# Three of nine dense column blocks in split fp32r parts, and every gathered dot beside the dense products: an expert mixer on one core

## The chip, the cores and the metric

The kernel runs on 1 core of one Trainium2 chip. Engines: PE (TensorE, matrix products), PEld (its weight loads), DVE (VectorE), ACT (ScalarE), POOL (GpSimd, which here issues the gathers by index), SP (SyncE, which issues the plain loads and stores). The metric is the device time of one execution in microseconds (us), as the median of several runs; lower is better. A time on the trace counts from the span's start.

## The reference, cut to what matters

One decoder layer for 256 prompt tokens and 32 sample tokens: an RWKV-7 and a sparse-attention token mixer, a norm, then a product-key expert mixer (PEER) and a last norm. The change lies in the PEER part of the prompt tokens, and in the last norm of the sample tokens:

```python
def peer_ffn(x, wq, subkeys, u_tab, v_tab):
    q = (xt @ wq).reshape(n, P_HEADS, 2, P_DKEY // 2)
    s = jnp.einsum('nhcd,hckd->nhck', q, subkeys)
    hv, hix = lax.top_k(s, P_TOPK)
    ...
    expert = jnp.take_along_axis(cand_e, tpos, axis=-1)
    gate = jax.nn.softmax(tv, axis=-1)
    h = jax.nn.gelu(jnp.einsum('cd,chkd->chk', xb, u_tab[eb]), approximate=False)
    return jnp.einsum('chk,chkd->cd', gb * h, v_tab[eb])
```

Each token chooses 8 x 16 = 128 of 16384 experts. For each it needs the dot product of its 2048 features with the expert's row of `peer_u`, a GELU, a gate, and then the sum of the experts' rows of `peer_v`, weighted by these.

## The kernel before, in words

All in one program: projections, RWKV chunks and attention first, then the queries and the choice of the experts, and from 1187.9 us (the first dense product) the three stages that matter here.

**Dense products beside dots.** The 2048 columns of `peer_u` are split. The last 9 blocks of 128 (`NDB = 9`) are taken densely: `dense(i1)` loads the rows of 128 experts, transposed, into a tile `ur` of 9 blocks (ring of `NUR = 5`), makes nine f32 products against the token features `Xfd` (128 x 256 each) into one PSUM bank `ph`, and ScalarE copies the result into a large table `AW`, which so holds, for each prompt token, the partial dot with every expert. There are 128 such steps. The first 7 blocks (`UG` = 896 columns) are taken by gather: `fetch` has POOL gather, for one slot of each of 128 tokens, the chosen expert's 896 columns into a tile of the ring `rows` (`NRW = 5`), and `dot` has VectorE multiply it with the tokens' features `X1a` and add up. There are 2 x 128 = 256 such dots, in two halves of 128 tokens. The loop asks for 1 or 2 dots per step (7 of 8 steps ask for 2), and what is left over after 128 steps is put into the first `NDL = 12` steps of the next stage. A gather waits until the dot five before it has released its tile.

**Spread sums.** 68 steps, pipelined over 64 groups of four tokens: `pick` builds one-hot rows (`oo`) on VectorE and transposes them on TensorE, `picked` multiplies `AW` with them to read out the chosen experts' partial dots, `product_of` reduces these on VectorE, `gated` applies gate and GELU, `scaled` scales the one-hots, `put` writes the weights back into `AW`. `table(t)` makes, for one half of the tokens, the transposed tables of indices, gates and gathered dots (`TB`) that `pick` needs. Beside it the sample tokens' experts are gathered whole (`smp_fetch`) and added up on TensorE (`smp_add`, weights `ws`), 32 times; after the loop their last norm follows, and 16 small stores.

**V products.** 128 blocks of 128 rows of `peer_v`: 1408 columns densely in split fp32r products, the other 640 by gather and VectorE.

The order on each engine is set by the framework's scheduler from a simulated time line, where nothing else fixes it. `keep_in_program_order` (`pin`) puts an instruction behind the one written just before it on its engine, and `issue_after` behind a given one. Each engine then works strictly in its order. Pools are stacks: `dp` (the dense tiles) and `kc` lie where `x4p` (the spread sums' tiles, `ws` and `oo` among them) comes later, and `up` (with `rows`, `x1a`) where the V products' tiles come; a tile in reused memory waits for the old one's last reader.

A split product writes each f32 operand as a rounded fp32r part plus its rest, and adds three of the four products of parts; the projections, the output projection and the V products do this already (lines 417 to 424, 1655 to 1661, 2059 to 2067).

Of the kernel before, what the change touches and what calls it, by code (L numbers as in the profile page):

```python
# [10 lines left out]
F32 = mybir.dt.float32  # L11
F32R = mybir.dt.float32r
I32 = mybir.dt.int32
U32 = mybir.dt.uint32
AF = mybir.ActivationFunctionType
OP = mybir.AluOpType
AX = mybir.AxisListType
PSUM = bass.MemoryType.PSUM
P = 128
# [3 lines left out]
NPR = 256  # L23
NEG = -1e30
ALPHA = 2.0 ** 0.25
# [23 lines left out]
NP1 = 8  # L49
NDW = 1  # L50
ND = 1
NDN = 7
NDL = 12
NUR = 5
NRW = 5
NDB = 9
UG = 128 * (16 - NDB)
WF = 3
PRO = 400
# [91 lines left out]
def hybrid_decode_step(ctx: ExitStack, tc: tile.TileContext, a, outs, dbg=None):  # L151
    nc = tc.nc
    ve, sc, pe, gp, sy = nc.vector, nc.scalar, nc.tensor, nc.gpsimd, nc.sync
# [35 lines left out]
    def bank(tag="pb"):  # L189
        places = [(pool, nm, n) for _, div in psum for t_, pool, nm, n in div for _ in range(n) if t_ == tag]  # L190
        turn[tag] = k = (turn.get(tag, -1) + 1) % len(places)
        pool, nm, n = places[k]
        return pool.tile([P, 512], F32, name=tag, tag=nm, bufs=n)
# [1248 lines left out]
    def norm_quarters(pool, x_, g_, b_, tag):  # L1442

        st, mv, rr, sq_ = pool([P, 6], "sst"), pool([P, 2], "smv"), pool([P, 1], "srr"), pool([P, 1], "ssq")
        ve.bn_stats(out=st, in_=x_)
        ve.bn_aggr(out=mv, in_=st)
        ve.tensor_tensor(sq_, mv[:, 0:1], mv[:, 0:1], OP.mult)
        ve.tensor_tensor(mv[:, 1:2], mv[:, 1:2], sq_, OP.add)
        pb = bank(tag)
        pe.matmul(pb[:, :2], C0("avg4"), mv, start=True, stop=True)  # L1450
        ve.tensor_copy(mv, pb[:, :2])
        ve.tensor_tensor(sq_, mv[:, 0:1], mv[:, 0:1], OP.mult)
        ve.tensor_tensor(mv[:, 1:2], mv[:, 1:2], sq_, OP.subtract)
        norm_row(pool, mv, rr)
        sc.activation(x_, x_, AF.Identity, bias=mv[:, 0:1], scale=rr)
        ve.tensor_tensor(x_, x_, g_, OP.mult)
        ve.tensor_tensor(x_, x_, b_, OP.add)
# [313 lines left out]
    TB = up([P, 4, NPR], "TB")  # L1771
    dp, kc, kq = (Pool(nm, "left") for nm in ("dp", "kc", "kq"))
    dp([P, NDB, P], "ur", bufs=NUR)
    Xfd = dp([P, NDB, NPR], "Xfd")
    SKT = kq([P, 16, P], "SKT")
    QP = kq([P, 16, NPR], "QP")

# [11 lines left out]
    def dot(n=1, upto=2 * P, keep=False, ahead=NRW):  # L1789

        for i in range(got[1], min(got[1] + n, upto)):
            t, s_ = dots[i]
            fetch(min(i + ahead, upto))
            r_, h_ = rows_.pop(i), HD[t][:, s_:s_ + 1]
            i_ = ve.scalar_tensor_tensor(r_, r_, 1.0, X1a[t], op0=OP.mult, op1=OP.mult, accum_out=h_)  # L1795
            if keep:
                tc.keep_in_program_order(i_)
            got[1] = i + 1

    def table(t):  # L1800

        pb = bank("pb")
        for q, (op_, v_) in enumerate(((OP.logical_shift_right, 7), (OP.bitwise_and, 127))):
            ii = up([P, P], "ii", I32)
            iff = ii.bitcast(F32)
            ve.tensor_scalar(ii, GI[t], v_, None, op0=op_)
            ve.tensor_copy(iff, ii)
            pe.transpose(pb[:, 128 * q:128 * q + 128], iff, ident)
        pe.transpose(pb[:, 256:384], GE[t], ident)
        pe.transpose(pb[:, 384:], HD[t], ident)  # L1810
        sc.copy(TB[:, :, P * t:P * t + P], pb.rearrange("p (a b) -> p a b", a=4))
# [36 lines left out]
        sample_formed()  # L1848
    sq_.close()
    kw_.close()  # L1850
    for q in range(0, NDB, 3):
        sc.copy(Xfd[:, q:q + 3, :], XT[:, 16 - NDB + q:19 - NDB + q, :])
    xq.close()
    kq.close()
    M_("peer")
# [6 lines left out]
    def dense(i1):  # L1862

        w = dp([P, NDB, P], "ur", bufs=NUR)
        sy.dma_start(w.rearrange("p k e -> p (k e)"), a["peer_u_t"][P * i1:P * i1 + P, :])
        ph = bank("ph")
        for e in range(NDB):
            mm = pe.matmul(ph[:, :NPR], w[:, e, :], Xfd[:, e, :], start=(e == 0), stop=(e == NDB - 1))  # L1868
        return mm, sc.copy(AW[:, i1 // 64, :, i1 % 64], ph[:, :NPR])  # L1869

    tabled = []
    for i1 in range(P):
        mm, end = dense(i1)
        n_ = ND + (i1 * NDN % 8 < NDN)
        dot(min(max(P - got[1], 0) or n_, n_))
        if got[1] >= P + 8 and not tabled:
            with tc.issue_after(mm.ins), tc.issue_after(end.ins):
                table(0)
            tabled.append(0)
    kc.close()  # L1880
    dp.close()
    if not tabled:
        dot(P - got[1])
        table(0)
    x4p, vr = Pool("x4", "left"), Pool("vr", "right")
    ig, vh2 = [GI[2], IG], vtab.rearrange("n (q c) -> (n q) c", q=2)
    banks(pt=2, px=2, pa=2, pb=1, fs=1)
# [60 lines left out]

    x4p([P, 4, P], "oT", bufs=2)
    ws = x4p([P, 32, 32], "ws")  # L1950
    ve.tensor_tensor(ws, C0("sum4")[:, None, :32].to_broadcast([P, 32, 32]), GE[2][:, :, None].to_broadcast([P, 32, 32]), OP.mult)
    fs, sr = bank("fs"), {}

    def smp_fetch(j):
# [5 lines left out]
    def smp_add(j):  # L1960
        for c in range(4):
            pin(pe.matmul(fs[32 * c:32 * c + 32, :], ws[:, j, :], sr[j, c // 2][:, 512 * (c % 2):512 * (c % 2) + 512],  # L1962
                          start=(j == 0), stop=(j == 31)))

    raw = {}

    def rows_load(k):

        raw[k] = (vp if k % 3 else vr)([P, FD], "v_", bufs=2 if k % 3 else 1)
        return sy.dma_start(raw[k], vtab[P * k:P * k + P, :FD])  # L1970

    left = 2 * P - got[1]
    for s_ in range(68):
        if s_ == 30:
            table(1)
        oT = pick(s_) if s_ < 64 else None
        if 3 <= s_ < 66 and s_ % 2:
            gated(s_ // 2 - 1)
        if s_ >= 4:
            put(s_ - 4)  # L1980
        if 0 <= s_ - 3 < 64:
            scaled(s_ - 3)
        if oT is not None:
            picked(s_, oT)
        if 0 <= s_ - 1 < 64:
            product_of(s_ - 1)
        if s_ < NDL:
            dot(-(-left * (s_ + 1) // NDL) + 2 * P - left - got[1], keep=True)
        for j in range(32):
            if s_ == NDL + j * (62 - NDL) // 32:  # L1990
                smp_fetch(j)
        for j in range(32):
            if s_ == NDL + 2 + j * (62 - NDL) // 32:
                smp_add(j)
        if s_ == 46:
            bs_, gs_, x_ = (xa_[:, 512 * n:512 * n + 512] for n in range(3))
            for q in range(4):
                r_, c_ = slice(32 * q, 32 * q + 32), slice(512 * q, 512 * q + 512)
                sy.dma_start(x_[r_, :], X1D[NPR:NT, c_])
                for t_, nm in ((gs_, "ln2_g"), (bs_, "ln2_b")):  # L2000
                    sy.dma_start(t_[r_, :], bass.AP(tensor=a[nm].tensor, offset=a[nm].offset + 512 * q, ap=[[0, 32], [1, 512]]))
        if s_ == 50:
            rows_load(0)
    pb = bank("pb")
    for t in range(2):
        pe.transpose(pb[:, 128 * t:128 * t + 128], TB[:, 2, P * t:P * t + P], ident)
        sc.copy(GE[t], pb[:, 128 * t:128 * t + 128])

    ve.scalar_tensor_tensor(x_, x_, ALPHA, fs, op0=OP.mult, op1=OP.add)
    norm_quarters(x4p, x_, gs_, bs_, "pb")  # L2010
    for q in range(4):
        for i in range(4):
            sy.dma_start(outs[1][:, i, 512 * q:512 * q + 512], x_[32 * q + 8 * i:32 * q + 8 * i + 8, :])
    x4p.close()
    up.close()
    banks(pj=2, pb=6)
# [136 lines left out]
```

## Time and profile before

| | |
|---|---|
| time, median of 3 runs | 2479.08 us (2474.55 to 2487.72) |
| the profiled execution | 2475.65 us |
| its span, mean granted TensorE clock | 2473.9 us, 0.95 |
| PE / PEld busy | 2255.7 us (91%) / 1886.1 us (76%) |
| DVE / ACT / POOL busy | 1745.4 us (71%) / 820.4 us (33%) / 1336.1 us (54%) |
| HBM read over the span | 665.69 MB |

How to read the lines: a group has line, engine, operation, tiles written <- tiles read, shape, and the count; then busy time in us, mean ns of one, and the engine's idle time before them, with what ended it. f32 matmuls show twice their number, since one is carried out in two passes. A window row has its bounds and length in us, each engine's busy time with its count of instructions, the granted clock (1.00 is full), the mean busy share of the 16 DMA engines, and GB/s; where windows of one line are asked for, only the engines that it runs on appear. A wait names the engine and tile that waited, and whom it waited for, with the total in us, the times, and the longest. A row of the timeline has start and duration in us.

### The profile page before, as it was taken

Reading aid. Unit: us, or ns where it says so; the run is one execution under the profiler, and the core shown is the slowest. Engines: PE = TensorE matmul, PEld = TensorE weight load, DVE = VectorE, ACT = ScalarE, POOL = GpSimd, SP = SyncE. Lnnn points to the kernel's source line nnn. Section 1 sums busy time; section 2 is a strip of 40 time slices with the busy share of each in tenths; the row PEclk is TensorE's granted clock in tenths of the full one; section 3 lists DMA queues with packets and bytes.
Section 4 is the critical chain, followed back from the end, with each engine's and each line's share of the span. In section 5 each row is a group of like instructions: output and inputs, shape, how many; then the busy total and the mean of one; then the engine's idle time right before and its main releaser. Section 6 shows DMA issues by size and latency. Waiting matters only on the chain.

```text
span 2473.9 us, 42694 instructions
## 1 busy us (share of the span) xinstructions
PE 2255.7 (91%) x15628; PEld 1886.1 (76%) x15628; DVE 1745.4 (71%) x3985; ACT 820.4 (33%) x1591; POOL 1336.1 (54%) x1419
## 2 busy tenths in 40 slices
PE   7979999997988997789999999995899799999996
PEld 7867898885645665578888888884777688888885
DVE  5789766555563446889856545556877799998888
ACT  3433222223341433220111111111777444443443
POOL 5678423233345005578666644655444588886672
PEclk9999999998896996899999999997999899999998
DMA  7777986449478984798699989995666699999994
GB/s 218 229 236 225 284 216 177 119 143 278 171 243 252 316 302 146 288 321 267 213 400 404 398 329 401 383 393 169 181 209 197 242 369 363 363 362 362 345 358 187
DMA packets 327602, 684.09 MB, mean 277 GB/s; under 512 B 82270, under 2 KB 200992, under 8 KB 326464
## 3 DMA queue, kind: packets, MB, share of 16 engines
q1 hardware_dynamic: 246176, 342.58, 41.7%
q0 software_dynamic: 81216, 338.78, 38.2%
q8 instruction: 123, 2.02, 0.3%
q14 instruction: 87, 0.71, 0.1%
HBM read 665.69 MB, written 23.88 MB: 279 GB/s over the span
## 4 chain that ended last, share of the span: by engine, by line
PE 46%; issue 14%; DVE 13%; POOL 11%; DMA 8%; ACT 2%; SPq 1%; POOLq 0%; DVEq 0%; ACTq 0%
PE pb L2067 19%; POOL rows L455 8%; PE pj L424 6%; PE pa L1661 3%; PE px L1910 2%; PE p L1081 2%; DVE sr L1557 2%; PE pa L1943 2%; DMA big<-in_state_rwkv 1%; PE ss L1498 1%; DMA co<-in_cache_cmp_kv,gidx 1%; PE pt L1902 1%; PE fs L1962 1%; DMA rows<-in_peer_u_g,gi 1%; DVE CA L478 1%
## 5 line engine op out<-in xcount | busy, mean ns | idle before, releaser
L1868 PE MATMUL ph<-Xfd,ur 128*128 128x256 f32 x2304 | 497.8, 379 | 0.0
L1868 PEld LDWEIGHTS ph<-Xfd,ur 128*128 128x128 f32 x2304 | 437.4, 190 | 59.5
L455 POOL DMA_INDIRECT rq<-in_peer_v_g,gi x256 | 378.5, 1479 | 142.0 <-DVE fP L2040 86.7
L455 POOL DMA_INDIRECT rows<-in_peer_u_g,gi x256 | 292.5, 1143 | 229.8 <-DVE rows L1795 199.5
L1795 DVE SCALAR_TENSOR_TENSOR rows<-rows,x1a 128x896 f32<-128x896 f32 x256 | 280.2, 1098 | 178.4 <-DMA rows<-in_peer_u_g,gi 178.0
L424 PE MATMUL pj<-XH,wl 128*128 128x288 f32 (+1 forms) x752 | 231.7, 308 | 14.9 <-DVE wl L419 8.5
L424 PE MATMUL pj<-XH,wh 128*128 128x288 f32 (+1 forms) x752 | 229.5, 305 | 15.2 <-DVE ss L754 6.9
L2040 DVE SCALAR_TENSOR_TENSOR fP<-rq,ge,fP 128x640 f32<-128x640 f32 x254 | 223.7, 881 | 5.7 <-DMA rq<-in_peer_v_g,gi 3.3
L424 PE MATMUL pj<-XL,wh 128*128 128x288 f32 (+1 forms) x752 | 225.9, 301 | 0.0
L2067 PE MATMUL pb<-vl,ah 128*128 128x512 f32 (+1 forms) x768 | 207.6, 378 | 1.3 <-DVE vl L2060 0.5
L1869 ACT COPY AW<-ph 128x256 f32<-128x256 f32 x128 | 77.2, 610 | 396.6 <-PE ph L1868 391.5
L2067 PE MATMUL pb<-vh,ah 128*128 128x512 f32 (+1 forms) x768 | 188.0, 380 | 22.1 <-ACT vh L2059 22.1
L2067 PE MATMUL pb<-vh,al 128*128 128x512 f32 (+1 forms) x768 | 205.8, 376 | 0.0
L417 ACT CAST wh<-wraw 128x512 fp32r<-128x512 f32 (+1 forms) x188 | 114.8, 616 | 228.9 <-PE pj L424 175.6
L2067 PEld LDWEIGHTS pb<-vh,ah 128*128 128x128 f32 x768 | 145.5, 196 | 44.9 <-ACT vh L2059 25.7
L478 DVE SCALAR_TENSOR_TENSOR CA<-co,wbc,CA 128x256 f32<-128x256 f32 x248 | 133.4, 575 | 48.7 <-DMA co<-in_cache_cmp_kv,gidx 48.7
L424 PEld LDWEIGHTS pj<-XH,wl 128*128 128x128 f32 (+1 forms) x752 | 143.8, 191 | 26.8 <-DVE wl L419 12.5
L2067 PEld LDWEIGHTS pb<-vl,ah 128*128 128x128 f32 x768 | 144.9, 195 | 24.2 <-DVE vl L2060 5.1
L424 PEld LDWEIGHTS pj<-XH,wh 128*128 128x128 f32 (+1 forms) x752 | 144.1, 192 | 21.4 <-DVE ss L754 7.3
L2067 PEld LDWEIGHTS pb<-vh,al 128*128 128x128 f32 x768 | 145.3, 195 | 19.4
L424 PEld LDWEIGHTS pj<-XL,wh 128*128 128x128 f32 (+1 forms) x752 | 144.2, 192 | 1.5 <-issue 1.2
L419 DVE TENSOR_TENSOR wl<-wraw,wh 128x512 fp32r<-128x512 f32 (+1 forms) x141 | 101.8, 731 | 44.4 <-ACT wh L417 43.8
(844 smaller groups left out, 4339.2 us busy)
## 6 DMA issues: line engine op xcount, KB each, us to landing
ur<-in_peer_u_t SPq DMA_DIRECT2D x128, 576.0 KB
wraw<-in_w_in SPq DMA_DIRECT2D x152, 256.0 KB
cw<-in_w_out SPq DMA_DIRECT2D x32, 512.0 KB
wraw<-in_w_out SPq DMA_DIRECT2D x32, 512.0 KB
wraw<-in_peer_wq SPq DMA_DIRECT2D x32, 512.0 KB
cw<-in_peer_wq SPq DMA_DIRECT2D x32, 512.0 KB
wraw<-in_w_in SPq DMA_DIRECT2D x64, 128.0 KB
co<-in_state_win_kv SPq DMA_DIRECT2D x16, 512.0 KB
```

Source lines behind the costliest of these rows:

```text
L417: sc.copy(wh[:, :, :n], w[:, :, :n])
L419: i_ = en.tensor_tensor(wl[:, :, :n], w[:, :, :n], wh[:, :, :n].bitcast(F32), OP.subtract)
L424: last[2] = pe.matmul(pb[:n, :nt], wi[:, k, :n], xi[(o + k) // 8][:, (o + k) % 8, :nt], start=(o + k == 0 and wi is wh and xi is xh), stop ...
L455: gp.indirect_dma_start(out=dst, out_offset=None, in_=rows_, in_offset=bass.IndirectOffsetOnAxis(ap=ix, axis=0))
L478: ve.scalar_tensor_tensor(d_, x_, w_, d_, op0=OP.mult, op1=OP.add)
L1081: pe.matmul(pb[hs[c], 64 * m:64 * m + 64], lhs(hs[c], m), rhs(hs[c], m), start=True, stop=True)
L1661: pe.matmul(acc[t], xi[:, e, P * t:P * t + P], wi[:, e, :], start=(k == e == n_ == 0), stop=(k == 6 and e == 1 and n_ == 2))
L1795: i_ = ve.scalar_tensor_tensor(r_, r_, 1.0, X1a[t], op0=OP.mult, op1=OP.mult, accum_out=h_)
L1868: mm = pe.matmul(ph[:, :NPR], w[:, e, :], Xfd[:, e, :], start=(e == 0), stop=(e == NDB - 1))
L1869: return mm, sc.copy(AW[:, i1 // 64, :, i1 % 64], ph[:, :NPR])
L2040: ve.scalar_tensor_tensor(fP[t], r_, w_, fP[t], op0=OP.mult, op1=OP.add)
L2067: pe.matmul(acc[3 * t + q][:, :n_], wi[:, P * t:P * t + P], xi[:, 512 * q:512 * q + n_], start=(k == 0 and wi is ah and xi is vh), stop=(k ...
```

## The change

Four things are altered together.

1. From step `NFB = 16` on, the first `NSP = 3` of the nine blocks of a dense step are computed as split products: ScalarE rounds the three weight blocks to fp32r, VectorE subtracts to get the rest (pinned), and nine fp32r matmuls follow the six f32 ones in the same bank. The token features get parts `XHd` and `XLd`. The ring `ur` shrinks from 5 to 3, and a ring `uhl` of 3 holds the parts.
2. The dots: 1 or 2 in turn for the first 16 steps, then 2 per step and pinned; the six left over come right behind the loop. None remain in the spread sums. `table(0)` is made once 152 dots are asked for, with four `ii` tiles in place of one; `table(1)` in step 20 in place of 30.
3. `ws` is made in step 1 of the spread sums, pinned, and the 32 additions of the sample lie in steps 3 to 58 in place of 14 to 62.
4. The sample's last norm and stores are issued in step 60 in place of after the loop.

```diff
-NDN = 7
-NDL = 12
-NUR = 5
+NDN = 8
+NUR = 3
+NSP = 3
+NFB = 16
...
-    Xfd = dp([P, NDB, NPR], "Xfd")
+    Xfd = dp([P, NDB - NSP, NPR], "Xfd")
+    XHd, XLd = dp([P, NSP, NPR], "XHd", F32R), dp([P, NSP, NPR], "XLd", F32R)
+    Xed = dp([P, NSP, NPR], "uhl", bufs=3)
...
-            ii = up([P, P], "ii", I32)
+            ii = up([P, P], "ii", I32, bufs=4)
...
-    for q in range(0, NDB, 3):
-        sc.copy(Xfd[:, q:q + 3, :], XT[:, 16 - NDB + q:19 - NDB + q, :])
+    for q, t_ in enumerate((Xed, Xfd[:, :3], Xfd[:, 3:])):
+        sc.copy(t_, XT[:, 16 - NDB + 3 * q:19 - NDB + 3 * q, :])
+    sc.copy(XHd, Xed)
...
-        for e in range(NDB):
-            mm = pe.matmul(ph[:, :NPR], w[:, e, :], Xfd[:, e, :], start=(e == 0), stop=(e == NDB - 1))
+        for e in range(NSP, NDB):
+            pe.matmul(ph[:, :NPR], w[:, e, :], Xfd[:, e - NSP, :], start=(e == NSP), stop=False)
+        if i1 < NFB:
+            for e in range(NSP):
+                mm = pe.matmul(ph[:, :NPR], w[:, e, :], Xed[:, e, :], start=False, stop=(e == NSP - 1))
+        else:
+            hl = dp([P, 2, NSP, P], "uhl", F32R, bufs=3)
+            sc.copy(hl[:, 0], w[:, :NSP, :])
+            tc.keep_in_program_order(ve.tensor_tensor(hl[:, 1], w[:, :NSP, :], hl[:, 0].bitcast(F32), OP.subtract))
+            for e in range(NSP):
+                for wi, xi in ((0, XHd), (0, XLd), (1, XHd)):
+                    mm = pe.matmul(ph[:, :NPR], hl[:, wi, e, :], xi[:, e, :],
+                                   start=False, stop=(e == NSP - 1 and wi == 1))
...
-    tabled = []
     for i1 in range(P):
+        if i1 == NFB:
+            ve.tensor_tensor(XLd, Xed, XHd.bitcast(F32), OP.subtract)
         mm, end = dense(i1)
-        n_ = ND + (i1 * NDN % 8 < NDN)
-        dot(min(max(P - got[1], 0) or n_, n_))
-        if got[1] >= P + 8 and not tabled:
+        n_ = ND + (i1 % 2 if i1 < NFB else 1)
+        dot(min(max(P - got[1], 0) or n_, n_), keep=i1 >= NFB)
+        if got[1] == P + 24:
             with tc.issue_after(mm.ins), tc.issue_after(end.ins):
                 table(0)
-            tabled.append(0)
...
+    def sample_out():
+
+        ve.scalar_tensor_tensor(x_, x_, ALPHA, fs, op0=OP.mult, op1=OP.add)
+        norm_quarters(x4p, x_, gs_, bs_, "pb")
+        for q in range(4):
+            for i in range(4):
+                sy.dma_start(outs[1][:, i, 512 * q:512 * q + 512], x_[32 * q + 8 * i:32 * q + 8 * i + 8, :])
+
...
-    left = 2 * P - got[1]
+    dot(2 * P - got[1])
+    at = lambda j: 2 + 55 * j // 31
+    bs_, gs_, x_ = (xa_[:, 512 * n:512 * n + 512] for n in range(3))
     for s_ in range(68):
-        if s_ == 30:
+        if s_ == 20:
             table(1)
...
-        if s_ < NDL:
-            dot(-(-left * (s_ + 1) // NDL) + 2 * P - left - got[1], keep=True)
+        if s_ == 1:
+            pin(ve.tensor_tensor(ws, C0("sum4")[:, None, :32].to_broadcast([P, 32, 32]),
+                                 GE[2][:, :, None].to_broadcast([P, 32, 32]), OP.mult))
         for j in range(32):
-            if s_ == NDL + j * (62 - NDL) // 32:
+            if s_ == at(j) - 1:
                 smp_fetch(j)
         for j in range(32):
-            if s_ == NDL + 2 + j * (62 - NDL) // 32:
+            if s_ == at(j) + 1:
                 smp_add(j)
-        if s_ == 46:
-            bs_, gs_, x_ = (xa_[:, 512 * n:512 * n + 512] for n in range(3))
+        if s_ == 24:
...
+        if s_ == 60:
+            sample_out()
...
-    ve.scalar_tensor_tensor(x_, x_, ALPHA, fs, op0=OP.mult, op1=OP.add)
-    norm_quarters(x4p, x_, gs_, bs_, "pb")
-    for q in range(4):
-        for i in range(4):
-            sy.dma_start(outs[1][:, i, 512 * q:512 * q + 512], x_[32 * q + 8 * i:32 * q + 8 * i + 8, :])
```

More of the change, by code (lines that the diff above doesn't have):

```diff
@@ L1866, in dense @@
         ph = bank("ph")
-        for e in range(NDB):
-            mm = pe.matmul(ph[:, :NPR], w[:, e, :], Xfd[:, e, :], start=(e == 0), stop=(e == NDB - 1))
+        for e in range(NSP, NDB):
[11 more added lines that the diff above has]
+                                   start=False, stop=(e == NSP - 1 and wi == 1))
         return mm, sc.copy(AW[:, i1 // 64, :, i1 % 64], ph[:, :NPR])
-    tabled = []
     for i1 in range(P):
+        if i1 == NFB:
+            ve.tensor_tensor(XLd, Xed, XHd.bitcast(F32), OP.subtract)
         mm, end = dense(i1)
-        n_ = ND + (i1 * NDN % 8 < NDN)
-        dot(min(max(P - got[1], 0) or n_, n_))
-        if got[1] >= P + 8 and not tabled:
+        n_ = ND + (i1 % 2 if i1 < NFB else 1)
+        dot(min(max(P - got[1], 0) or n_, n_), keep=i1 >= NFB)
+        if got[1] == P + 24:
             with tc.issue_after(mm.ins), tc.issue_after(end.ins):
                 table(0)
-            tabled.append(0)
     kc.close()
     dp.close()
-    if not tabled:
-        dot(P - got[1])
-        table(0)
     x4p, vr = Pool("x4", "left"), Pool("vr", "right")
@@ L1950, in hybrid_decode_step @@
     ws = x4p([P, 32, 32], "ws")
-    ve.tensor_tensor(ws, C0("sum4")[:, None, :32].to_broadcast([P, 32, 32]), GE[2][:, :, None].to_broadcast([P, 32, 32]), OP.mult)
     fs, sr = bank("fs"), {}
```

## The prediction

> **What bounds the kernel now.** All durations are from one profiled execution, 2475.65 us with a span of 2473.9 us. I read the page first, then the stretch of the dense products.
>
> ```profile
> L1868 PE MATMUL ph<-Xfd,ur 128*128 128x256 f32 x2304 | 497.8, 379 | 0.0
> L1868 PE MATMUL ph<-Xfd,ur x2304: 379/379/382, 1187.9 to 1685.4; 128*128 128x256 f32 x192
> L1795 DVE SCALAR_TENSOR_TENSOR rows<-rows,x1a 128x896 f32<-128x896 f32 x256 | 280.2, 1098 | 178.4 <-DMA rows<-in_peer_u_g,gi 178.0
> L1795 DVE DVE_READ_ACCUMULATOR rows<-rows,x1a 128x1 f32 x256 | 21.1, 83 | 0.0
> ur<-in_peer_u_t SPq DMA_DIRECT2D x128, 576.0 KB
> ```
>
> TensorE never stands here: 2304 matmuls in 497.8 us, 216 ns each, two per f32 block of 256 columns, so 18 x 216 = 3.89 us per step. A dot takes VectorE 1.098 + 0.083 = 1.18 us, but it waits for gathered rows. The windows of the dots' line give, for each stretch, its length, VectorE's busy time in dots, their instructions (two per dot), granted clock, DMA share and GB/s:
>
> ```profile
> 1187.00:1220.00 33.00, 3.12 (x3) 1.00 0.55 177
> 1220.00:1250.00 30.00, 13.82 (x26) 1.00 0.97 363
> 1250.00:1300.00 50.00, 29.71 (x54) 1.00 1.01 400
> 1300.00:1450.00 150.00, 88.97 (x162) 1.00 1.01 399
> 1450.00:1500.00 50.00, 18.25 (x35) 1.00 0.86 311
> 1650.00:1686.00 36.00, 6.59 (x12) 1.00 0.56 216
> 1686.00:1712.30 26.30, 19.29 (x35) 0.63 0.75 248
> 1712.30:1755.00 42.70, 14.32 (x28) 0.83 0.57 171
> ```
>
> The DMA engines are full (share 1.01, 399 to 400 GB/s) and give a dot every 50 / 27 = 1.85 us. So two things are tight together: TensorE, and transfers. By 1686 some 225 of 256 dots are done; (35 + 28) / 2 = 31 are left, and they hold the spread sums until 1755. Two of the holes in the transfers have names in the waits and the timeline of VectorE:
>
> ```profile
> DVE ii L1806 <- PE pb L1808: 23.4, 3, 16.5
> 1678.06 1.23 DVE L1951 TENSOR_TENSOR ws<-CT,ge 128x1024 f32<-128x1024 f32 x1 [18.17 <-PE ph L1868]
> 1680.21 1.22 DVE L1898 TENSOR_TENSOR oo<-CT,TB 128x1024 f32<-128x1024 f32 x1
> 1712.44 1.22 DVE L1898 TENSOR_TENSOR oo<-CT,TB 128x1024 f32<-128x1024 f32 x1
> 1915.65 1.22 DVE L1898 TENSOR_TENSOR oo<-CT,TB 128x1024 f32<-128x1024 f32 x1
> ```
>
> The single `ii` buffer holds VectorE 16.5 us (the 0.86 window), and `ws`, in memory of the dense tiles, 18.2 us (the 0.56 window); dots queue behind both. Step 2 of the spread sums picks only at 1712.44, 27 us after the dense end; the last of 64 picks is at 1915.65.
>
> **The change part by part.** *The split.* From step 16 on, 6 blocks stay f32, 12 x 216 = 2.59 us, and three become nine fp32r matmuls of 256 columns. The nearest rows are the projection's fp32r matmuls of 288 columns, TensorE's timeline at full clock:
>
> ```profile
> 40.03 0.30 PE L424 MATMUL pj<-XH,wh 128*128 128x288 f32 x1
> 40.16 0.29 PE L424 MATMUL pj<-XL,wh 128*128 128x288 f32 x1
> ...
> 41.09 0.29 PE L424 MATMUL pj<-XH,wl 128*128 128x288 f32 x1
> ```
>
> Eight starts in 1.06 us, 133 ns. By columns 256 take 118; 133 is the upper end, and I take 120: 9 x 120 = 1.08 us in place of 6 x 216 = 1.30. A step falls to 3.67 us (3.65 to 3.79).
>
> *What it adds to ScalarE and VectorE.* A cast and a subtraction of 128x384 per step. Rows of the same two operations:
>
> ```profile
> L417 ACT CAST wh<-wraw 128x512 fp32r<-128x512 f32 x184 | 112.8, 618 | 228.2 <-PE pj L424 175.6 <-DMA wraw<-in_w_in 38.9 <-issue 5.0
> L419 DVE TENSOR_TENSOR wl<-wraw,wh 128x512 fp32r<-128x512 f32 x138 | 100.2, 735 | 44.4 <-ACT wh L417 43.8
> L1656 DVE TENSOR_TENSOR wl<-wraw,wh 128x1024 fp32r<-128x1024 f32 x24 | 30.8, 1284 | 21.5 <-ACT wh L1655 21.4
> L1869 ACT COPY AW<-ph 128x256 f32<-128x256 f32 x128 | 77.2, 610 | 396.6 <-PE ph L1868 391.5 <-DVE HV L1364 5.1
> ```
>
> The line through 735 and 1284 ns gives 0.60 us for 384 elements. VectorE then has 2 x 1.18 + 0.60 = 2.96 us a step, ScalarE at most 0.61 + 0.62: both fit under 3.67, at no cost while they are not held by a wait.
>
> *Transfers per step.* 576 KiB of columns (590 kB) and now two gathers of 128 x 896 x 4 bytes (917 kB): 1507 kB, at 399 GB/s 3.78 us. This is above 3.67, so transfers set the pace, and a faster TensorE alone brings nothing.
>
> *The new order.* From step 16 each subtraction is pinned behind the dots of the step before, on VectorE, and TensorE's split matmuls wait for it. Step 17's stands behind 28 dots (2 ahead of the loop, 24 of the first 16 steps, 2 of step 16). TensorE ends step 15 at 1187.9 + 16 x 3.89 = 1250.1, when (3 + 26) / 2 = 14 dots are done. Fourteen more at 1.85 us, or at 26.3 / 17.5 = 1.50 us as in 1686 to 1712 without column loads, end at about 1272 (nearer the second, as the three column buffers soon are full), while TensorE is through what it can do at 1256: it stands some 16 us. Then 110 steps at 3.78 us are 416, less 3 us for two column tiles already landed (2 x 590 kB / 399): the last subtraction at 1685, the dense end at 1686, as now. The gain of the split is eaten by dots that are now done inside: **0 us** at the dense end. Its ends: -12 at TensorE's own 3.67 us a step, +41 at the 363 GB/s of the row with share 0.97 (4.15 us). I take 3.78, since 150 us of the same two kinds of transfer ran at it.
>
> *The dots behind it.* Eight dots follow the last subtraction (two of its step, six left), five landed at 1.18, three at 1.50: 10 us. The first pick is pinned behind them: 1696. `ws` and the second `ii` no longer block.
>
> *The spread sums.* Windows of the picks' line, then of the sample's matmuls (eight per addition), with the same stretch:
>
> ```profile
> 1754.40:1854.40 100.00, 38.93 (x32) 1.00 0.66 205
> 1754.40:1854.40 100.00, 20.24 (x152) 2.99 (x152) 1.00 0.66 205
> ```
>
> 32 steps and 19 additions in 100 us; an addition is 20.24 / 19 = 1.065 us, so a bare step is 2.49 us. 63 steps and all 32 additions: 157 + 34 = 191 us, since the dots no longer stand between. Add `ws` at 1.2 us and a cold start: TensorE stands about 10 us, and the granted clock answers to that:
>
> ```profile
> 1700.00:1726.00 26.00, 9.97 (x41) 8.51 (x42) 21.48 (x58) 3.15 (x8) 17.79 (x14) 0.50 0.74 249
> 1942.00:1949.00 7.00, 4.99 (x13) 4.22 (x14) 2.51 (x3) 2.74 (x2) 5.78 (x5) 0.52 0.99 378
> ```
>
> About 7 us at half clock cost 3.5 us. Last pick so far: 1696 + 191 + 5 = 1892.
>
> *The sample's norm in step 60.* Everything pinned after it on VectorE, TensorE and ScalarE queues behind its chain, and the pick of step 61 with them. Its rows now:
>
> ```profile
> 1917.90 0.69 DVE L2009 SCALAR_TENSOR_TENSOR x1a<-x1a,fs 128x512 f32<-128x512 f32 x1 [1.03 <-PE fs L1962]
> 1930.80 6.42 SPq L2013 DMA_DIRECT2D out<-x1a  x16
> 1931.17 2.71 PE L2067 MATMUL pb<-vh,ah 128*128 128x512 f32 x6 [4.22 <-ACT vh L2059]
> 1937.90 0.36 SPq L1970 DMA_DIRECT2D v__18333<-in_peer_v  x1
> 1944.01 2.40 PE L2067 MATMUL pb<-vh,ah 128*128 128x512 f32 x5 [6.96 <-ACT vh L2059]
> ```
>
> It runs 12.9 us; earlier steps cover two steps of it (5 us), so it costs 8 (5 to 13): last pick at 1900, 16 us ahead of 1915.65. In return, the row loads at 1937.90 no longer stand behind 16 stores on SP; TensorE's 7.0 us gap goes, and with it the second half-clock stretch, half of 5 us: -9. The first V product stays 15.5 us behind the last pick. From 1944 on nothing changes.
>
> **Sum:** 0 - 16 - 9 = -25, so 2475.65 - 25 = 2451. The runs' median, 2479.08, lies 3.4 above the profiled time, so I say 2452 for a median.
>
> **The rivals.** (1) *Transfers fall below the pace, slower.* Now five column buffers and free dots keep requests queued; then there are three, freed only when TensorE, ScalarE and VectorE are through, and a late gather stops the subtraction, the matmul, and so the next column load. For it: the 16.5 us hold of VectorE took the share to 0.86. Against: up to five gathers remain in flight, and 150 us at 1.01. It decides from 3.78 + (25 + 12) / 110 = 4.12 us a step; at a share of 0.90 (355 GB/s) a step is 4.25, +52 us, 2503. The Trainium skill (DMA: Bandwidth & Descriptors, Specifications) states about 358 GB/s as the HBM limit of a core; by it a step of 1507 kB would be 4.21 us and the time 2498, an estimate from that page; the 399 GB/s over 150 us here speaks against it. Chance 0.15. (2) *The end gives nothing back.* The norm holds step 61 for its full 13 us, and the V products still wait, for AW or for rows: 0 - 11 + 0, 2465. For it: 12.9 us is a chain of single operations that wait on each other. Chance 0.20. (3) *VectorE catches up early.* No standing at step 17, TensorE-bound: 62 + 112 x 3.67 = 473, dense end 1661; the dots, by transfers, still end about 1684, so -12 more: 2439. Against: only 14 dots are done at 1250. Chance 0.08. That the split does not shorten a step at all (133 ns) is inside the main case, since transfers set the pace.
>
> **How the numbers follow.** The main case, 2440 to 2466, has 0.57. Faster by over 0.5% (12 us, about what a measurement of this kernel can tell) are the main case and (3), 0.65; (2) lies 10 us below the profiled time, no change, 0.20; (1) is slower, 0.15. The range 2436 to 2484 holds the main case, (2) and (3) and the mild part of (1), up to 4.08 us a step; it leaves out the rest of (1).
>
> **What would show it.** Right: after about 1250 a TensorE gap near 16 us and half clock; steps then 3.7 to 3.85 us at DMA share 1.0; fp32r starts 118 to 133 ns apart; dense end 1680 to 1692, all dots done 8 to 15 us later; 64 picks within 205 us; a hole of some 8 us between the picks of steps 60 and 61; the second row block without a 7 us wait. Wrong: steps above 4 us with a share below 0.95 (rival 1), a V start no earlier than 1925 (rival 2), or no gap after 1250 (rival 3).

## The result and the profile after

The changed kernel takes 2462.38 us (median of 10 runs, 2455.15 to 2469.18) where the kernel before took 2479.62 (10 runs, 2469.30 to 2494.98), measured beside it: a ratio of 0.9928, 95% interval 0.9903 to 0.9953, some 17 us faster. Its profiled execution took 2468.47 us, with a span of 2466.7 us and a mean clock of 0.943.

First the rows by tile of the changed kernel. They give count, duration (min/median/max, ns) and first and last start in us: the query products ahead of the stage (`pj`), the dense products (`ph`) and the picks (`oo`).

```profile
L1827 PE MATMUL pj<-XT,wraw x512: 379/379/634, 1063.1 to 1188.3; 128*128 128x256 f32 x171
L1872 PE MATMUL ph<-Xfd,ur x1536: 377/379/796, 1189.7 to 1700.5; 128*128 128x256 f32 x192
L1882 PE MATMUL ph<-XHd,uhl x672: 277/283/579, 1265.6 to 1702.5; 128*128 128x256 f32 x168
L1910 DVE TENSOR_TENSOR oo<-CT,TB x64: 1217/1219/1222, 1713.6 to 1920.4; 128x1024 f32<-128x1024 f32 x64
```

The dense product ends at 1702.8, 17 us later than before, not sooner. The first pick stands at 1713.6, 1.1 us behind the 1712.44 of the second pick before; the last at 1920.4, 4.7 us later. Yet the span is 7.2 us shorter, and the first query product already starts late: it is at 1055.2 in the kernel before (next fence), at 1063.1 here. Among all profiled executions of this study it lies between 1046.3 and 1067.4, in code that no kernel here changes. So profiles are compared from that product on: 1418.7 us to the end before, 1403.6 after, **15.1 us less**, near the 17 of the medians. Each kernel has one profile, and e4 below, in which the one instruction it was to move stayed where it was, differs from the changed kernel by 6.8 us in this count: smaller differences between two profiles prove little.

The same row of the kernel before:

```profile
L1824 PE MATMUL pj<-XT,wraw x512: 379/379/667, 1055.2 to 1186.5; 128*128 128x256 f32 x171
```

And the longest of its TensorE's waits from 1055 to 1187 (total us, times, longest):

```profile
PE pj L1824 <- DMA wraw<-in_peer_wq: 8.2, 3, 3.7
```

From the first query product to the first dense product it is 132.7 us before (1055.2 to 1187.9) and 126.6 after (1063.1 to 1189.7). No step of the prediction has this. Before, five loads of dense blocks stood in SyncE's queue ahead of 21 loads of query weights, and TensorE waited 8.2 us for such weights; with three buffers only three loads stand there, and the waits for weights are gone (e1 and e7 below separate the buffers from the split).

The stage itself, by windows of the dots' line (length, VectorE busy in dots with instructions, clock, DMA share, GB/s):

```profile
1220.00:1250.00 30.00, 10.34 (x16) 0.84 0.64 244
1250.00:1300.00 50.00, 30.03 (x55) 0.90 0.97 359
1300.00:1450.00 150.00, 88.77 (x161) 1.00 1.02 405
1450.00:1500.00 50.00, 27.38 (x52) 0.97 1.01 389
1500.00:1650.00 150.00, 86.03 (x157) 1.00 1.01 394
1650.00:1686.00 36.00, 21.48 (x40) 1.00 1.02 408
1686.00:1713.00 27.00, 16.78 (x31) 0.90 0.93 341
```

Transfers are full from 1300 on, and the dots come no faster than before (161 instructions in 150 us, 162 then). What is new is that the two holes, 0.86 from 1450 and 0.56 from 1650, are filled: so all dots fit in. The windows from 1220 to 1300 are poorer than before (244 and 359 GB/s, 363 and 400 then). TensorE's waits in the whole stage:

```profile
PE ph L1882 <- DVE uhl L1879: 12.6, 2, 11.6
PE ph L1872 <- DMA ur<-in_peer_u_t: 8.5, 10, 3.3
PE ph L1872 <- ACT AW L1884: 8.2, 2, 7.6
```

The two long ones in its timeline, with ScalarE's row at the first:

```profile
1223.39 0.70 ACT L1427 ACTIVATE ge<-ge 128x128 f32<-128x128 f32 x2 [19.03 <-DVE ge L1426]
1224.62 5.36 PE L1872 MATMUL ph<-Xfd,ur 128*128 128x256 f32 x12 [7.57 <-ACT AW L1884]
1277.77 0.79 PE L1882 MATMUL ph<-XHd,uhl 128*128 128x256 f32 x2 [11.57 <-DVE uhl L1879]
```

Before, TensorE did not stand at all. Now it stands 7.57 us since the gates' exponentials sit in ScalarE's queue in front of the copies that free the `ph` banks, and wait 19 us for VectorE's choice of the keys. ScalarE waited there before as well (17 us), but the dense product started later against that choice (its last reduction ended 35.5 us behind the first dense product, now 43.6), and five banks covered the wait. Counted from the first query product, that reduction starts equally late in both kernels, 167 us before (1222.3) and 169 after (1232.2). VectorE is busy until then (29.95 of 30 us from 1190 to 1220), so the sooner start of the dense product does not bring the dots forward. The 11.57 us are the first subtraction's, queued behind 26 dots.

Last, from the timeline, the picks of steps 60 and 61 with the norm's first multiplication by the gains between them, and the start of the V products:

```profile
1904.72 1.22 DVE L1910 TENSOR_TENSOR oo<-CT,TB 128x1024 f32<-128x1024 f32 x1
1911.70 0.69 DVE L1457 TENSOR_TENSOR x1a<-x1a 128x512 f32<-128x512 f32 x1 [0.88 <-ACT x1a L1456]
1913.03 1.22 DVE L1910 TENSOR_TENSOR oo<-CT,TB 128x1024 f32<-128x1024 f32 x1
...
1933.35 2.71 PE L2084 MATMUL pb<-vh,ah 128*128 128x512 f32 x6 [2.47 <-ACT ah L2073]
1938.61 1.44 PE L2084 MATMUL pb<-vh,ah 128*128 128x512 f32 x6
```

The hole of 8.31 us between two picks is the norm; the second row block follows the first without a gap and starts 18.3 us behind the last pick, where it was 28.4 (1915.65 to 1944.01).

The stretches of every kernel of this study, in us, each from the first start to the next; the last column is the sum from the first query product to the span's end:

| kernel | query to dense | dense to first pick | first to last pick | to V's 2nd block | to the end | sum |
|---|---|---|---|---|---|---|
| before (from its 2nd pick) | 132.7 | 524.5 | 203.2 | 28.4 | 529.9 | 1418.7 |
| changed | 126.6 | 523.9 | 206.8 | 18.3 | 528.1 | 1403.6 |
| e1 no split | 127.2 | 524.8 | 204.9 | 18.4 | 527.0 | 1402.3 |
| e2 split alone | 126.7 | 519.7 | 205.5 | 27.7 | 529.5 | 1409.1 |
| e3 norm behind | 126.5 | 525.2 | 196.7 | 27.0 | 530.7 | 1406.1 |
| e4 gates later | 127.6 | 520.1 | 203.2 | 19.4 | 526.5 | 1396.8 |
| e5 half gathers, split | 127.5 | 481.3 | 202.5 | 17.0 | 528.6 | 1356.9 |
| e6 half gathers, no split | 126.6 | 534.1 | 205.8 | 18.4 | 526.5 | 1411.4 |
| e7 no split, 5 buffers | 131.9 | 513.1 | 206.0 | 18.7 | 526.8 | 1396.6 |
| e8 e7, gates later | 132.1 | 511.8 | 205.8 | 18.3 | 526.8 | 1394.8 |
| e9 e7, loads behind | 133.2 | 507.7 | 204.5 | 17.0 | 527.9 | 1390.2 |
| e10 e5, f32 matmuls | 128.0 | 507.7 | 201.7 | 17.0 | 528.1 | 1382.5 |
| e11 f32 matmuls | 127.5 | 549.5 | 207.6 | 18.5 | 526.6 | 1429.7 |
| e12 e9, dots sooner | 131.0 | 507.1 | 205.2 | 18.8 | 526.6 | 1388.7 |

Before, 14 dots of 256 were still undone at the second pick, and the third column holds 63 picks, not 64. So the 15.1 us are 6.1 ahead of the dense product, 0.6 in it, 10.1 behind the last pick and 1.8 in V, less 3.6 in the picks, where 8.3 us of norm came in and the dots went out.

### The profile page after: what moved, and what is told of

It is laid out like the page before. It is cut to its first block, busy times and chain, and to the rows that moved or that the text cites. A ratio compares the mean times of both kernels' runs of the same rounds, so it can differ in the third digit from the quotient of the medians.

```text
span 2466.7 us, 43713 instructions
## 1 busy us (share of the span) xinstructions
PE 2243.8 (91%) x15964; PEld 1888.4 (77%) x15964; DVE 1799.0 (73%) x4098; ACT 859.7 (35%) x1704; POOL 1319.1 (53%) x1419
## 4 chain that ended last, share of the span: by engine, by line
PE 49%; POOL 13%; issue 12%; DVE 12%; DMA 11%; ACT 2%; SPq 1%; POOLq 0%; DVEq 0%; ACTq 0%
PE pb L2084 19%; POOL rows L456 8%; PE pj L425 7%; PE px L1922 3%; DMA rows<-in_peer_u_g,gi 3%; PE pa L1662 2%; PE pa L1955 2%; DVE sr L1558 2%; PE p L1082 2%; DMA co<-in_cache_cmp_kv,gidx 2%; PE pt L1914 2%; PE ss L1499 1%; PE fs L1973 1%; DMA big<-in_state_rwkv 1%; DVE CA L479 1%
## 5 line engine op out<-in xcount | busy, mean ns | idle before, releaser
L456 POOL DMA_INDIRECT rows<-in_peer_u_g,gi x256 | 269.6, 1053 | 209.8 <-DVE rows L1798 193.0
L1872 PE MATMUL ph<-Xfd,ur 128*128 128x256 f32 x1536 | 359.5, 384 | 16.8 <-DMA ur<-in_peer_u_t 8.5
L1872 PEld LDWEIGHTS ph<-Xfd,ur 128*128 128x128 f32 x1536 | 286.5, 192 | 55.9 <-DMA ur<-in_peer_u_t 10.9
L2057 DVE SCALAR_TENSOR_TENSOR fP<-rq,ge,fP 128x640 f32<-128x640 f32 x254 | 223.7, 881 | 6.6 <-DMA rq<-in_peer_v_g,gi 4.2
L2084 PEld LDWEIGHTS pb<-vh,al 128*128 128x128 f32 x768 | 145.2, 194 | 19.4
L1882 PE MATMUL ph<-XHd,uhl 128*128 128x256 f32 x672 | 148.5, 314 | 12.6 <-DVE uhl L1879 12.6
## 6 DMA issues: line engine op xcount, KB each, us to landing
wraw<-in_w_in SPq DMA_DIRECT2D x64, 128.0 KB
```

What stands on the lines that cost most here:

```text
L456: gp.indirect_dma_start(out=dst, out_offset=None, in_=rows_, in_offset=bass.IndirectOffsetOnAxis(ap=ix, axis=0))
L1872: pe.matmul(ph[:, :NPR], w[:, e, :], Xfd[:, e - NSP, :], start=(e == NSP), stop=False)
L1882: mm = pe.matmul(ph[:, :NPR], hl[:, wi, e, :], xi[:, e, :], start=False, stop=(e == NSP - 1 and wi == 1))
L2057: ve.scalar_tensor_tensor(fP[t], r_, w_, fP[t], op0=OP.mult, op1=OP.add)
L2084: pe.matmul(acc[3 * t + q][:, :n_], wi[:, P * t:P * t + P], xi[:, 512 * q:512 * q + n_], start=(k == 0 and wi is ah and xi is vh), stop=(k ...
```

## The experiments

The theory at the outset: transfers set the pace of the dense stage, so the split buys nothing there and the gain is of the end (A in the expectations). The rival: TensorE's shorter step is what gains (B). All ratios are to the kernel before, measured beside each set. The sets ran on different chips, so kernels of two sets compare by their ratios.

**e1: no split.** All nine blocks in f32 in every step; all else as changed.

```diff
+NSF = 128
...
-        if i1 < NFB:
+        if i1 < NSF:
```

> The changed kernel, with all nine blocks of every dense step in f32 (no split); dots, ws and norm as changed. Theory A (transfers and the dots set the pace from step 16 on, the split buys no time): TensorE needs 3.89 us a step again but waits for no subtraction, dense end near 1695, all dots done by 1700 to 1714 as in the changed kernel: 2457 to 2467, within 5 us of the changed kernel's 2462. Rival B (the split is what gains): 112 x 0.22 = 25 us slower than the changed kernel, 2487.

Measured 2465.12 us, 0.9943 (0.9917 to 0.9969); the changed kernel has 0.9928 (0.9903 to 0.9953). The split is worth 0.9 us of the dense stage here (524.8 against 523.9), less than two profiles differ by; the time is as A has it. But it was not TensorE's own pace that filled this stage: a step took (1709.9 - 1185.2) / 128 = 4.10 us, or 4.05 without the stop of 6.8 us at the gates, not 3.89. Its dense rows by tile:

```profile
L1873 PE MATMUL ph<-Xfd,ur x1536: 379/379/796, 1185.2 to 1708.2; 128*128 128x256 f32 x192
L1876 PE MATMUL ph<-uhl,ur x768: 379/379/380, 1187.8 to 1709.5; 128*128 128x256 f32 x192
```

And TensorE's wait for dense blocks in this stage:

```profile
PE ph L1873 <- DMA ur<-in_peer_u_t: 8.6, 12, 2.3
```

The dots were all done by 1696, 14 us ahead of the dense product: the gathers took more than their share of the transfers, and dense blocks came late. From 1300 to 1650 this kernel issued 86 loads of dense blocks and 192 gathers, the changed one 92 and 184, at 397 and 398 GB/s.

**e2: the split alone**, with its three buffers, in the kernel before (dots, `ws`, table and norm as before).

```diff
-NUR = 5
+NUR = 3
+NSP = 3
+NFB = 16
...
```

> The kernel before, with the split of three blocks from step 16 on and nothing else (three column buffers, subtraction pinned as in the change; dots, ws, table and norm as before). Theory A: dots are still left for the spread sums, and TensorE now stands for subtractions behind late dots: 2475 to 2492, no faster than before (2480). Rival B: 15 to 25 us faster than before, 2455 to 2465.

2467.26 us, 0.9951 (0.9922 to 0.9979). Theory A said no gain, and it is wrong there: the split with its buffers gains about as much as the rest does without the split. By the table 6.0 us of its 9.6 lie ahead of the dense product: that is mostly the three buffers (e1 against e7), not the split. Its dense stage also holds a stop of 14.35 us, behind a load of V rows as in e7, so its 519.7 us are not the split's worth alone.

**e3: the norm behind the loop**, as before the change.

```diff
-        if s_ == 60:
-            sample_out()
...
+    sample_out()
```

> The changed kernel, with the sample's norm and stores behind the loop again. Theory A (the move costs about 8 us at step 61 and gives about 9 back at the first V products): within 5 us of the changed kernel, 2457 to 2468; the hole between the picks of steps 61 and 62 goes, the wait of 7 us before the second row block comes back. Rival C (the hole costs and nothing is given back): 8 to 13 us faster than the changed kernel, 2449 to 2454.

2467.14 us, 0.9944 (0.9919 to 0.9969). The picks fall from 206.8 to 196.7 us and the way to V grows from 18.3 to 27.0: moving the norm is nearly even (225.1 against 223.7 for the two together), as theory A has it. Without the move the picks take 6.5 us less than in the kernel before (203.2 there); with the 6.2 us ahead of the dense product that is nearly all of the 12.6 us that e3's profile gains. No run takes apart what went out of the picks: dots, `ws`, table and the spread of the sample's additions.

**e4: the gates written in dense step 12.**

```diff
-    for t in range(2):
-        gates(t, up, TV[t])
...
+        if i1 == 12:
+            for t in range(2):
+                gates(t, up, TV[t])
```

> The changed kernel, with the gates of the prompt tokens written in dense step 12 in place of ahead of the loop, so that the first table copies on ScalarE don't queue behind its exp that waits 19 us for VectorE. Theory A: TensorE's 7.6 us hold near 1217 goes; column loads start earlier, but the dots still come late, so 2 to 7 us faster than the changed kernel, 2455 to 2460, with TensorE standing longer at step 17 instead. Rival D (the hold is what made the dense stretch end 17 us later than forecast): 8 to 12 us faster, 2450 to 2454.

2464.80 us, 0.9930 (0.9903 to 0.9957): no different. ScalarE's timeline says why:

```profile
1206.27 0.69 ACT L1427 ACTIVATE ge<-ge 128x128 f32<-128x128 f32 x2 [19.00 <-DVE ge L1426]
1206.87 1.03 ACT L1882 COPY AW<-ph 128x256 f32<-128x256 f32 x2
```

The exponentials are still issued in front of the copies and wait 19 us. The place in the text did not move them in the queue, so this run tells nothing of the stop. It tells how far two profiles of nearly one program differ: 3.8 us in the stage and 3.6 in the picks.

**e5 and e6: half of the gathers**, with the split and without. Every second dot uses the row before, so half of the second set of products is left out.

```diff
+            if i % 2:
+                rows_[i] = rows_[i - 1]
+            else:
...
-            fetch(min(i + ahead, upto))
+            fetch(min(i + 2 * ahead - 1, upto))
```

> The changed kernel with every second gather of the dots left out (each row is used by two dots, so half of the second set of products is wrong data by intent and the transfers of the gathers are halved; all instructions of TensorE, VectorE and ScalarE stay). Theory T, the transfers set when the picks begin: with 589.8 + 458.8 kB a step nothing waits for DMA, TensorE runs at its own 3.67 us a step from block 16 on, dense product and dots together take 16 x 3.89 + 112 x 3.67 + some 15 us of stops = 488 to 500 us from the first dense product to the first pick, against 523.9 us in the changed kernel: 2434 to 2442 us. Theory E, the engines set it (the copies and subtractions of the split, VectorE's dots): step stays at 3.80 us, stage stays at 515 to 524 us, 2455 to 2463 us.

2410.84 us, 0.9743 (0.9703 to 0.9783), and a stage of 481.3 us, below even theory T's 488 to 500. The split matmuls' row by tile:

```profile
L1885 PE MATMUL ph<-XHd,uhl x672: 277/283/470, 1245.1 to 1654.0; 128*128 128x256 f32 x168
```

And a window of TensorE (length, busy time, clock, DMA share, GB/s):

```profile
1300.00:1450.00 150.00, 150.00 (x861) 1.00 0.86 288
```

TensorE never stands in the window, and the split steps take (1654.0 - 1.0 - 1245.1) / 111 = 3.67 us (the last start is some 1.0 us into the split part of its step). With all gathers they took 3.81: (1702.5 - 1.0 - 1282.6) / 110, from the second split step, which begins these matmuls at 1282.6. No instruction of TensorE, VectorE or ScalarE went; gathers did, and with them their issue on GpSimd; but GpSimd was busy in only 80.81 of these 150 us in the changed kernel with all gathers, at a DMA share of 1.02. The stop at the first subtraction went too, as the first 26 dots come sooner.

> The same half of the gathers left out, in the changed kernel without any split (all nine column blocks in f32, as in the first run of this study). Theory T: TensorE alone sets the pace, 128 x 3.89 us + 7 us of stops, and the dots end with it: 505 to 510 us to the first pick against 524.8 us with all gathers, 2445 to 2452 us; the split is then worth 8 to 20 us, while with all gathers it was worth 0.9 us of this stage. Theory E: as with all gathers, 520 to 525 us and about 2465 us, and no difference beyond 3 us between the two kernels with half of the gathers.

2467.81 us, 0.9951 (0.9927 to 0.9974): as slow as with all gathers, but not for the reason of theory E. Windows of the dots' line:

```profile
1300.00:1450.00 150.00, 143.65 (x271) 0.95 0.94 339
1500.00:1650.00 150.00, 13.45 (x26) 1.00 0.56 187
```

And TensorE's wait for dense blocks:

```profile
PE ph L1876 <- DMA ur<-in_peer_u_t: 21.2, 11, 14.3
```

Without a subtraction in VectorE's queue nothing holds the dots to the pace of the dense steps. They ran as fast as VectorE can (143.65 of 150 us), were all but two done by 1512, and in that time the dense blocks came late. e6 is no measure of the split without transfers; e10 is.

**e7 and e8: no split, five buffers**, for which the memory of the parts leaves room. e8 has e4's edit besides, which again did not move the exponentials (ScalarE issues them at 1222.3 in front of the copies), so it is a second look at e7.

```diff
-NUR = 3
+NUR = 5
...
-    XHd, XLd = dp([P, NSP, NPR], "XHd", F32R), dp([P, NSP, NPR], "XLd", F32R)
-    Xed = dp([P, NSP, NPR], "uhl", bufs=3)
+    Xed = dp([P, NSP, NPR], "uhl", bufs=1)
```

> The changed kernel without the split and with five buffers for the dense blocks, as before the change; all gathers stay, dots still lie beside the dense products. Theory T1, the transfers are full but their order is at fault (without the split the dots were done 15 us ahead of the dense product, and its step was 4.04 us in place of 3.89, waiting for dense blocks): with two more blocks ahead the step goes back to 3.89 to 3.93 us, the dense product ends after 500 to 508 us and the dots within 8 us of that, the first pick comes 508 to 515 us after the first dense product, 2449 to 2456 us. Theory T2, only the sum of the bytes counts: the blocks come earlier and the rows by as much later, the dots end 518 to 525 us after the start, and the time stays at 2462 to 2467 us.

2453.46 us, 0.9895 (0.9865 to 0.9925). Time and stage are as T1 has them: steps of 3.89 us, dots and dense product done together, 513.1 us to the first pick. The dense product itself took 512.8 us, not 500 to 508, by one stop; the timeline of TensorE and SyncE around it:

```profile
1207.39 0.33 SPq L1868 DMA_DIRECT2D ur<-in_peer_u_t  x1
1227.48 0.33 SPq L1986 DMA_DIRECT2D v__17743<-in_peer_v  x1
1227.91 3.37 SPq L1868 DMA_DIRECT2D ur<-in_peer_u_t  x5
1238.59 5.46 PE L1871 MATMUL ph<-Xfd,ur 128*128 128x256 f32 x12 [10.69 <-DMA ur<-in_peer_u_t]
```

For 20 us SyncE issues nothing: a load of the first V rows stands in its queue and waits 19.7 us for GpSimd's casts of indices (tile `gi`), with five dense blocks behind it.

> The kernel with five buffers and no split, and besides the gates' exponentials written behind dense block 12, so that the copies of the dense product do not wait behind them. Theory T1: the stop of 7 us at the start goes too, dense product done after 498 to 503 us, first pick 504 to 512 us, 2444 to 2452 us. Theory T2: the stop at the start is covered by the transfers, 2460 to 2467 us, as with the stop.

2453.44 us, 0.9885 (0.9847 to 0.9923), with the same stop of 10.7 us.

**e9: e7 with that load, and the norm's, queued behind the dense blocks.**

```diff
-            rows_load(0)
+            pin(rows_load(0))
```

> The kernel with five buffers and no split stood 10.69 us once, at 1228: its SyncE queue held a load of the first V rows behind ten dense blocks, which waited for memory, and five dense blocks behind that. Here this load and the sample norm's loads are queued behind all dense blocks. Theory S, the stop is that load's: the gap is gone, the dense product takes 128 x 3.89 us = 498 to 502 us (512.9 with the stop), the dots, with the transfers full, end 503 to 509 us after the start, the first pick comes at 504 to 510 us, 2445 to 2451 us. Theory B, the bytes alone set the first pick: dense product ends earlier, the dots do not, first pick 511 to 515 us after the start, 2452 to 2456 us.

2454.49 us, 0.9873 (0.9827 to 0.9919). In the profile theory S holds: TensorE's row runs without a stop and the first pick comes 507.7 us after the first dense product, 5.4 sooner than in e7. The median doesn't show these 5 us: 2454.49 lies in theory B's range, and its interval is wider than the difference. That the stop was the load's is shown; that its end saves time is not. The dense row by tile, 128 steps in 498.3 us (1182.6 to 1681.0, 1.7 us behind the last start shown):

```profile
L1871 PE MATMUL ph<-Xfd,ur x1536: 379/379/483, 1182.6 to 1679.3; 128*128 128x256 f32 x192
```

**e10: e5 with f32 matmuls.** The parts are made and not used; TensorE multiplies all nine blocks in f32. As in e5, half of the second products are left out.

```diff
-                for wi, xi in ((0, XHd), (0, XLd), (1, XHd)):
-                    mm = pe.matmul(ph[:, :NPR], hl[:, wi, e, :], xi[:, e, :],
-                                   start=False, stop=(e == NSP - 1 and wi == 1))
+                mm = pe.matmul(ph[:, :NPR], w[:, e, :], Xed[:, e, :], start=False, stop=(e == NSP - 1))
```

> The kernel with the split and every second gather of the dots left out (half of the products are wrong data by intent), and in it the nine matmuls of the split columns written as three in f32; the copy and the subtraction that make the parts stay and are not used. Against the same kernel with the split's matmuls it differs in TensorE's work alone; the subtraction still ties the dots to the dense blocks, which was missing where no split at all let the dots run ahead and starve the dense blocks. Theory T: the step goes from 3.67 to 3.89 us, 481.3 us to the first pick become 504 to 509 us, 2433 to 2440 us, against 2410.8 us. Theory U, it was the pacing by the subtraction and not the shorter matmuls that made that kernel fast: 2408 to 2416 us.

2438.27 us, 0.9826 (0.9768 to 0.9884); 507.7 us to the first pick against 481.3. Where transfers are not full, the split's matmuls are worth 26 us of the stage, of which 112 x 0.22 = 25 us are TensorE's shorter steps. This is theory T.

**e11: the same edit with all gathers.**

> The changed kernel with all gathers, and the nine matmuls of the split columns written as three in f32, the copy and the subtraction left in place and not used: TensorE's part of the split alone is undone. Theory T, the transfers set the first pick: dense step 3.89 to 3.95 us in place of 3.80, dots end at most 4 us later, first pick 522 to 530 us after the first dense product against 523.9 us, 2461 to 2470 us. Theory E, TensorE's step sets it: 112 x 0.22 us = 25 us later, 545 to 550 us, 2484 to 2490 us.

2487.65 us, 1.0018 (0.9988 to 1.0047). Theory T named 522 to 530 us of stage; it was 549.5, E's number. But E's reason isn't there: f32 steps take 3.89 us with all gathers in e7 and e9. Here they take 4.09 from step 20 on. Two of its waits from 1300 to 1650:

```profile
DVE uhl L1879 <- ACT uhl L1878: 100.4, 80, 3.7
PE ph L1872 <- DMA ur<-in_peer_u_t: 10.5, 12, 2.1
```

And a window of all engines (PE, PEld, DVE, ACT, POOL, then clock, DMA share, GB/s):

```profile
1300.00:1450.00 150.00, 145.69 (x664) 124.38 (x663) 98.73 (x186) 33.69 (x72) 86.53 (x75) 1.00 0.99 375
```

VectorE waits 100 us for casts (8.9 us in the changed kernel, in the same stretch), which ScalarE issues behind the copy that waits for the matmuls. So dots, and the gathers behind them, are tied to TensorE's steps, and the transfers fall to 375 GB/s. e1 is this kernel without the casts and subtractions of the steps, and its stage is 524.8 us: so the f32 matmuls alone do not make the 25 us; with them, the casts and subtractions do. That they do it by this tie is argued, not shown: no run takes the tie away and leaves them.

**e12: e9 with two dots a block from block 0 on** (and e4's edit, which again did not move the exponentials: ScalarE issues them at 1220.53, after a wait of 19.10 us).

```diff
-        n_ = ND + (i1 % 2 if i1 < NFB else 1)
+        n_ = ND + 1
```

> No split, five buffers, the loads queued behind the dense blocks, the gates' exponentials behind dense block 12, and two dots a block from block 0 on in place of one and two in turn: all that the runs have shown to cost something in the dense stage, taken out together. Transfers run at 400 GB/s from some 40 us after the start: dense product done after 498 to 500 us, dots by 500 to 506 us, first pick 501 to 507 us, 2442 to 2449 us. If the earlier dots come no earlier, because VectorE still has the choice of the keys until 30 us after the start, it is as the kernel with the loads behind, 2445 to 2451 us.

2445.22 us, 0.9843 (0.9795 to 0.9890): faster than both kernels; its interval lies wholly below the changed kernel's, while it overlaps those of e7, e8 and e9. It has no split at all. The two dots a block bought nothing that shows against e9: 507.1 us to the first pick where e9 has 507.7, and 501.9 us of dense product where 498 to 500 were expected. The sum from the first query product is 14.9 us below the changed kernel's, 16.8 of that in the dense stage, with 4.4 given back by the five loads ahead of the query weights.

## Why the prediction was right, and where it was wrong

Its sign and its range held: 2452 was said, 2436 to 2484, and 2462.38 came. It sized the gain at 25 us; 17 came. Its sum with its own 3.4 us for a median gives 2475.65 - 25 + 3.4 = 2454, where it says 2452. By its own steps:

- *A step of 3.67 us, and transfers above it at 3.78.* Right on both, and the load-bearing point: 3.67 us in e5, 3.81 with all gathers, at 394 to 405 GB/s over 150 us. By the rule of the Trainium skill (DMA: Bandwidth & Descriptors, Specifications) of about 358 GB/s, which was a rival, the time would have been 2498 us, an estimate from that page; the trace disagrees with it here. The same page (Bandwidth) has 425 GB/s for large transfers of a lone core and about 358 for each of two that stream together; with one core running, 394 to 405 lie between.
- *0 us at the dense end.* This step failed: the dense product took 513.1 us from its start (1189.7 to 1702.8), 15 more than the 498 that it was to keep. The start was right: the subtraction that binds was put at step 17, behind 28 dots, 84 us after the first dense product; it was step 16's, behind 26, and came at 1277.2, 87.5 us after. The dots were on time for it: 14 were done 194.8 us after the first query product (1257.9), where the prediction read 14 from the kernel before (1250, as far from its own). TensorE stood 11.57 us there and 7.57 behind the gates, against 16 in the sum. What failed is the length from there on, 422.7 us to the last subtraction (1699.9) where 413 were said. It was 111 steps of 3.81 and not 110 of 3.78, which makes some 7 us, and the credit of 3 us for two tiles already landed did not come: TensorE waited 8.5 us for `ur`. The dense product then ended 2.9 us behind the last subtraction, not 1.
- *Eight dots, 10 us.* Eight followed, and took 13.2 (1700.4 to 1713.6). They waited for gathers, 2.87 us the longest time. So the stage took 523.9 us to the first pick, 15.8 more than said (1696 less 1187.9).
- *The picks.* 204 us with 8 of them for the norm at step 60; 206.8, with 8.31 us between the two picks. Right; against e3 the norm costs 10.1, and e3's 196.7 are the 196 that the sum has without it.
- *V, -9 us.* Right, as the gap ahead of the second block went (7.6 us less between the two blocks) and 1.8 us behind it. The first V product did not stay 15.5 us behind the last pick, as said, but came 13.0 behind it, 2.5 us that were not in the sum.
- *What no step had:* 6.1 us ahead of the dense product, from two loads fewer in front of the query weights. It is the buffers: e7, with five and f32 like e1, has 131.9 us there and e1 127.2; TensorE waits 6.4 us for query weights in e7, 0.3 in e1. That is 4.7 of the 6.1; the rest stays open.

Counted from the first query product the sum was missed by some 10 us: 15.8 too few in the dense stage and 2.8 in the picks, against 6.1 ahead of the stage and 2.9 behind the picks that were gained beyond the forecast. That the total came so near is in part luck: gains that no step had made up for half of the miss. Part of both may be one thing, as the dots began no sooner when the dense product did: to the first pick, it is 650.5 us from the first query product, where the sum has 640.8.

Of the rivals, the slower one (transfers below pace) shows only in small: 359 GB/s from 1250 to 1300 and 341 at the end. The second, with no gain at the end, came near in time (2465), but not by its mechanism, as V starts 10 us sooner. The third, a stage bound by TensorE, is what e5 shows once gathers are halved.

The theory that the split buys nothing holds against e1, the same kernel without parts (0.9 us of the stage). It doesn't hold against e11, where the parts stay and only the matmuls change (25.6 us). Both hold together: with f32 matmuls, making the parts costs this stage 24.7 us (e11 against e1), and with the parts made, the shorter matmuls give that back. And the split had a price: its parts took the memory of two dense buffers, and without the split those are worth 11 us of the stage (e7 against the changed kernel), 16 to 17 with the loads queued right (e9, e12), less the 4 to 7 that they cost ahead of it. No run has the split with more than three buffers.

## What to carry to other kernels

Before making an engine faster in a stage, read what share the DMA engines have there: at 1.0 a shorter step only turns into waits, and by the profiles, two more buffers for dense blocks were worth more here. Follow each prefetch through its queue to the work in front of it and behind it: two loads more ahead of other weights cost 4 to 7 us, and one early load that had to wait held TensorE 11 us, of which its removal gave 5 back in the profile of the stage and none in the median. An edit to the program's order is tested only if the timeline shows that the instruction moved.

## What the runs showed of the hardware

The DMA share alone does not tell the rate: 0.94 came with 339 GB/s where gathers ran ahead of the dense blocks (e6), 0.99 with 375 (e11), 1.02 with 405 (changed). An fp32r matmul of 256 columns takes (3.67 - 12 x 0.216) / 9 = 0.120 us by e5's step. Behind both stops the changed kernel's TensorE ran slowly for some microseconds. Twelve f32 passes, which usually take 2.75 us, took 5.36 behind the stop of 7.57 us (1224.62 above). Behind that of 11.57 us the seven split matmuls took 1.66 us from 1277.77 to the start of the next step, 0.24 each, and twelve passes then took 3.49:

```profile
1263.21 2.75 PE L1872 MATMUL ph<-Xfd,ur 128*128 128x256 f32 x12
1279.43 3.49 PE L1872 MATMUL ph<-Xfd,ur 128*128 128x256 f32 x12
```

The mean granted clock was 0.84 from 1220 to 1250 and 0.90 from 1250 to 1300, and 1.00 from 1300 to 1450.
